# A mixture-of-experts layer in which 32 of 256 tokens take their down products from gathered rows on VectorE

## The chip, the core and the metric

The kernel runs on one core of a Trainium2 chip. The metric is the device time in microseconds of one execution, the median of several. TensorE (PE, with PEld for its weight loads), VectorE (DVE), ScalarE (ACT), GpSimd (POOL) and the queue of SyncE (SP) each run their own instructions in order and wait for one another by semaphores.

## The reference, cut to what matters

Two transformer blocks over 256 tokens of width 1024. The first ends with PEER, a retrieval of experts, which the change is about:

```
sub_scores = einsum('thpc,hpkc->thpk', qry, sub_keys)   # 8 heads x 2 halves x 128 keys
top_s, top_i = top_k(sub_scores, 16)                    # 32 searches of 128 per token tile pair
best_s, best_c = top_k(sums of 16 x 16 pairs, 16)       # 8 heads: 128 experts per token
gate = softmax(best_s)
u = expert_down[ids]                                    # 128 of 16384 rows, each 1024 wide
act = gelu(einsum('pd,ped->pe', x, u)) * gate
y = einsum('pe,ped->pd', act, expert_up[ids])
```

## The kernel before

The retrieval gathers nothing. It multiplies all 256 tokens with all 16384 rows of `expert_down`, in 128 units of 128 rows (`downs`): a unit loads 512 KB (`wst`), splits it into a rounded part on ACT (`whi`, L78) and a rest on DVE (`wlo`, L80), and PE runs 24 matmuls, three for each of eight slices of the width, into a PSUM tile `dn` of 128 x 256 (`mm3`, L113 to L115; the tokens are `hh` and `hl`, split likewise). `wst`, `whi` and `wlo` have three buffers each. ACT puts gelu of `dn` into `G[:, j, :]`.

The choice of experts becomes a gate matrix. `tops` and `select` search on DVE (`top16`, five instructions; 32 searches over 128 keys, then 16 over 136 pair sums, a token tile being 128 tokens), turn pair numbers into indices by one-hot blocks (L730 on ACT, L731 to L738 on DVE), and `softmax` transposes indices and gates to `ijgT`. `gates` takes four tokens at a time: ACT builds `A` and DVE `B` (one-hot rows, `B` times the gate), PE multiplies them into `gp`, and DVE multiplies the units of G that are there with it; units that come later are multiplied in `downs`. `ups` then multiplies G with all of `expert_up`, into `y`.

Three generators set the order: queries and the first 44 units beside the searches; 80 units beside the 64 gate batches; the last 4 beside `ups`. `interleave` takes from the stream that is least far. A scheduler of the tile framework then sets each engine's order by what it expects an instruction to cost; on the chip each engine follows that order.

Of the kernel before, what the change touches and what calls it, by code (L numbers as in the profile page):

```python
# [8 lines left out]
F32 = mybir.dt.float32  # L9
F32R = mybir.dt.float32r  # L10
BF16 = mybir.dt.bfloat16
I32 = mybir.dt.int32
U16 = mybir.dt.uint16
AF = mybir.ActivationFunctionType
OP = mybir.AluOpType
# [28 lines left out]
def interleave(*streams):  # L44


    gens = [[e[0], e[1], e[2] if len(e) > 2 else 0.0] for e in streams]
    while gens:
        gens.sort(key=lambda e: e[2])
        e = gens[0]  # L50
        try:
            e[2] += (next(e[0]) or 1.0) / e[1]
        except StopIteration:
            gens.remove(e)


class Core:
# [15 lines left out]
    def unit(self, ap, n=1024):  # L73
        nc = self.nc
        st = self.wst.tile([P, 1024], F32, tag="wst", name="wst")
        nc.sync.dma_start(st[:, :n], ap)
        hi = self.whi.tile([P, 1024], F32R, tag="whi", name="whi")
        self.last_hi = nc.scalar.activation(hi[:, :n], st[:, :n], AF.Copy)  # L78
        lo = self.wlo.tile([P, 1024], F32R, tag="wlo", name="wlo")
        nc.vector.tensor_tensor(lo[:, :n], st[:, :n], hi[:, :n], OP.subtract)  # L80
        return hi, lo

    def unit_hi(self, ap):
# [76 lines left out]
    def rsqrt(self, pool, ms, scale, n, tag, tiles=None):  # L160

        nc = self.nc
        p = ms.shape[0]
        r, t = tiles or [pool.tile([P, n], F32, tag=tag + x, name=tag + x) for x in "rt"]
        self.act_le(r[:p], ms, AF.Ln, scale=scale, bias=self.eps[:p])
        self.act_le(r[:p], r[:p], AF.Exp, scale=-0.5)

        self.rs_act = nc.scalar.activation(t[:p], r[:p], AF.Square, scale=float(np.sqrt(0.5 * scale)))
        nc.vector.scalar_tensor_tensor(t[:p], ms, EPS / scale, t[:p], OP.add, OP.mult)
        self.rs_dve = nc.vector.scalar_tensor_tensor(r[:p], t[:p], 1.5, r[:p], OP.subtract, OP.mult, reverse0=True)  # L170
        return r[:p]

# [412 lines left out]


    def peer(self):
        nc, a = self.nc, self.a
        h = (self.hh, self.hl)
        with ExitStack() as st:  # L590
            pg = self.pool("pg", 1, stack=st)
            tm = self.pool("pgt", 2, stack=st)
# [38 lines left out]
            nc.vector.tensor_copy(iob, self.iota[:, :16])  # L631
            ijgT = [pg.tile([P, T], F32, name=f"ijgT{x}") for x in range(3)]

            def downs(js, state):
                for j in js:
                    w = self.unit(a["down"][j])
                    ps = dps.tile([P, T], F32, tag="d", name="dn")
                    self.mm3(ps, w, h)
                    b = 4 * state["batches"]
                    if b == 0:  # L640
                        nc.scalar.activation(G[:, j, :], ps, AF.Gelu)  # L641
                    else:
                        t = tm.tile([P, T], F32, tag="gel", name="gel", bufs=1)
                        if b < T:
                            nc.scalar.activation(G[:, j, b:], ps[:, b:], AF.Gelu)
                        self.last_gelu = nc.scalar.activation(t[:, :b], ps[:, :b], AF.Gelu)
                        nc.vector.tensor_tensor(G[:, j, :b], G[:, j, :b], t[:, :b], OP.mult)
                    state["downs"] = j + 1
                    yield

            def queries():
                def scores(hp):
                    q = qry[hp % 2]
                    sp = gps.tile([P, 512], F32, tag="g", name="sp")
                    for tt in range(2):
                        nc.tensor.matmul(sp[:, tt * P:(tt + 1) * P], q[:, tt * P:(tt + 1) * P], subk[:, hp, :], start=True, stop=True)
                    for tt in range(2):
                        nc.scalar.activation(S[tt][:, hp, :], sp[:, tt * P:(tt + 1) * P], AF.Copy)

                first = []  # L660
                for hp in range(2):
                    first.append((dps.tile([P, T], F32, tag="d", name="qp"), self.unit(a["wq"][hp])))
                self.mm3s(first, h)
                for hp in range(16):
                    if hp < 2:
                        ps = first[hp][0]
                    else:
                        w = self.unit(a["wq"][hp])
                        ps = dps.tile([P, T], F32, tag="d", name="qp")
                        self.mm3(ps, w, h)  # L670
                    nc.scalar.activation(qry[hp % 2], ps, AF.Copy)
                    if hp:
                        scores(hp - 1)
                    yield
                scores(15)

# [25 lines left out]
            def select():  # L702
                for tt in range(2):
# [23 lines left out]
                    for s in range(2):  # L727
                        if s == 0:
                            yield 3.0
                        self.after(nc.scalar.activation(abx, ab[s].unsqueeze(3).broadcast_to([P, 8, 16, 16]), AF.Copy), self.last_hi)  # L730
                        nc.vector.tensor_tensor(eq, abx,  # L731
                                                iob.unsqueeze(1).unsqueeze(1).broadcast_to([P, 8, 16, 16]), OP.is_equal)
                        yield 2.2
                        nc.vector.tensor_tensor(eq, eq, idxb[tt][:, :, s, :].unsqueeze(2).broadcast_to([P, 8, 16, 16]), OP.mult)

                        for w in (8, 4, 2):
                            nc.vector.tensor_tensor(eq[:, :, :, :w], eq[:, :, :, :w], eq[:, :, :, w:2 * w], OP.add)
                        nc.vector.tensor_tensor(ijg[tt][s].rearrange("p (h k) -> p h k", h=8), eq[:, :, :, 0], eq[:, :, :, 1], OP.add)  # L738
                        yield 2.4
                    g = ijg[tt][2].rearrange("p (h k) -> p h k", h=8)  # L740
                    nc.vector.tensor_tensor(g, best[tt], best[tt][:, :, 0:1].broadcast_to([P, 8, 16]), OP.subtract)
                    if tt:
# [4 lines left out]
            def gates(state):  # L747
                iT, jT, gT = ijgT
                for b in range(T // 4):
                    gp = gps.tile([P, 4, P], F32, tag="g", name="gp")  # L750

                    A = tm.tile([P, 4, P], F32, tag="A", name="A", bufs=3)
                    for q in range(4):
                        nc.scalar.activation(A[:, q, :], self.iota, AF.Abs, bias=iT[:, 4 * b + q:4 * b + q + 1])  # L754
                    nc.scalar.activation(A, A, AF.Relu, bias=1.0, scale=-1.0)
                    for q in range(4):
                        t = 4 * b + q
                        B = tm.tile([P, P], F32, tag="B", name="B", bufs=4)
                        nc.vector.tensor_scalar(B, self.iota, jT[:, t:t + 1], gT[:, t:t + 1], OP.is_equal, OP.mult)  # L759
                        nc.tensor.matmul(gp[:, q, :], A[:, q, :], B, start=True, stop=True)  # L760
                    gv = gp.rearrange("p t j -> p j t")
                    n = state["downs"]
                    ts = slice(4 * b, 4 * b + 4)
                    if n:
                        nc.vector.tensor_tensor(G[:, :n, ts], G[:, :n, ts], gv[:, :n, :], OP.mult)
                    if n < NS:
                        nc.scalar.activation(G[:, n:, ts], gv[:, n:, :], AF.Copy)
                    state["batches"] = b + 1
                    yield
# [33 lines left out]
            def take(g, n):  # L803
                for _ in range(n):
                    try:
                        next(g)
                    except StopIteration:
                        return
                    yield
# [9 lines left out]
            interleave((chain(qs, take(dn, self.cfg["sel"])), 14.0 + self.cfg["sel"]), (chain(tops(), select()), 80.0))  # L819
            for x in range(3):  # L820
                self.dump(f"ijgT{x}", ijgT[x])
            interleave((take(dn, self.cfg["gate"]), float(self.cfg["gate"])), (gates(state), 64.0))
            rest = NS - state["downs"]
            def gate2():

# [25 lines left out]
            for c in range(8):  # L851
# [8 lines left out]
                if c == 5:  # L860
                    third = self.unit_hi(a["win2"][0])
            self.pre[0] = self.unit_lo(*third, self.last_hl)
            self.dump("x2", self.xT)
            r = self.rsqrt(None, ms[:, :T], 1.0 / D, T, "", [self.rb, Gf[:, 2 * T:3 * T]])


    def block2(self, peer=True):
# [494 lines left out]
def layouts(i):  # L1362
# [29 lines left out]
    o["subk"] = f("peer_sub_keys").reshape(16, P, P).transpose(2, 0, 1).reshape(P, 2048)  # L1392
    o["down"] = f("peer_down").reshape(P, P, 8, P).transpose(1, 3, 2, 0).reshape(P, P, 1024)
    o["up"] = f("peer_up").reshape(P, P, 1024).transpose(1, 0, 2)
    w = f("w_in_2")
    kv = lambda b: w[:, 512 + 128 * b:640 + 128 * b]

# [29 lines left out]
```

## Time and profile before

| | |
|---|---|
| median of 3 runs | 1391.29 us (1390.59 to 1391.79) |
| the profiled execution | 1389.8 us, span 1388.0 |
| busy PE / PEld / DVE / ACT / POOL | 1353.5 / 1256.4 / 991.9 / 816.9 / 4.6 us |
| mean granted TensorE clock | 0.993 of 2.4 GHz |
| data by DMA | 248.53 MB, 179 GB/s |

The span runs from the first to the last instruction. A busy share is an average; the rows below show the stretches of the retrieval. Matmuls overlap, so a matmul's time in a row is longer than the distance to the next; PE's pace is read from the starts.

### The profile page before, as it was taken

To read this page: it belongs to the slowest core of one execution; us is meant where nothing else is said; L and a number is where in the kernel's file an instruction comes from. 1 tells how busy PE (TensorE), PEld (TensorE's weight loads), DVE (VectorE), ACT (ScalarE), POOL (GpSimd) and SP (SyncE) were. 2 spreads that over 40 slices of the span, in tenths; PEclk is the share of its full clock that TensorE was granted. 3 is DMA by queue.
4 is the path that set the end of the run, shared out by engine and by line. 5 is a ranking of instruction groups with operands and counts; after the bars stand their busy time and mean duration, and the time that the engine had idled before them with its cause. 6 is when DMAs were issued, how large, how long until landed. Compare 5 with 4: busy or idle time off the path is not lost.

```text
span 1388.0 us, 24896 instructions
## 1 busy us (share of the span) xinstructions
PE 1353.5 (98%) x9598; PEld 1256.4 (91%) x9598; DVE 991.9 (71%) x2050; ACT 816.9 (59%) x1577; POOL 4.6 (0%) x17
## 2 busy tenths in 40 slices
PE   6999979999999999999999999999998999999998
PEld 6988879999999999999988888888888988999998
DVE  6788979996766667777776666665667787755555
ACT  3466545446778888888545555455556565644443
POOL 0000000000000000000000000000001000000000
PEclk9999999999999999999999999999999999999999
DMA  8686344456544444444566666566654731455554
GB/s 340 223 318 245 105 150 149 149 179 195 180 154 141 150 152 140 151 152 141 181 212 212 215 211 212 196 195 188 194 178 153 213 122 62 138 186 185 182 185 129
DMA packets 65828, 248.53 MB, mean 179 GB/s; under 512 B 7568, under 2 KB 8464, under 8 KB 62766
## 3 DMA queue, kind: packets, MB, share of 16 engines
q1 hardware_dynamic: 65709, 246.94, 54.2%
q8 instruction: 75, 1.23, 0.4%
q14 instruction: 44, 0.35, 0.1%
HBM read 245.87 MB, written 1.05 MB: 178 GB/s over the span
## 4 chain that ended last, share of the span: by engine, by line
PE 89%; DVE 7%; ACT 2%; DMA 1%; issue 1%; SPq 0%; DVEq 0%; ACTq 0%
PE y L785 8%; PE y L787 8%; PE y L786 8%; PE dn L113 8%; PE dn L114 8%; PE dn L115 8%; PE gp L760 4%; DVE wlo L80 2%; PE fu L115 2%; PE fu L114 2%; PE fu L113 2%; PE yf L1287 2%; PE yf L1288 2%; PE yf L1289 2%; PE pj L113 2%; PE pj L115 2%
## 5 line engine op out<-in xcount | busy, mean ns | idle before, releaser
L80 DVE TENSOR_TENSOR wlo<-wst,whi 128x1024 fp32r<-128x1024 f32 (+1 forms) x410 | 499.9, 1220 | 203.1 <-ACT whi L78 202.4
L78 ACT ACTIVATE whi<-wst 128x1024 fp32r<-128x1024 f32 (+1 forms) x410 | 431.1, 1052 | 261.2 <-PE dn L114 77.0
L113 PE MATMUL dn<-hh,whi 128*128 128x256 f32 x1024 | 295.8, 289 | 1.1 <-ACT G L641 1.1
L115 PE MATMUL dn<-hh,wlo 128*128 128x256 f32 x1024 | 290.2, 283 | 2.8 <-DVE wlo L80 2.8
L114 PE MATMUL dn<-hl,whi 128*128 128x256 f32 x1024 | 289.5, 283 | 0.0
L785 PE MATMUL y<-whi,aa 128*128 128x512 f32 x512 | 200.0, 391 | 0.0
L787 PE MATMUL y<-whi,aa 128*128 128x512 f32 x512 | 199.3, 389 | 0.0
L786 PE MATMUL y<-wlo,aa 128*128 128x512 f32 x512 | 199.3, 389 | 0.0
L115 PEld LDWEIGHTS dn<-hh,wlo 128*128 128x128 f32 x1024 | 195.9, 191 | 3.7 <-DVE wlo L80 3.6
L113 PEld LDWEIGHTS dn<-hh,whi 128*128 128x128 f32 x1024 | 196.2, 192 | 1.7 <-ACT G L641 1.5
L114 PEld LDWEIGHTS dn<-hl,whi 128*128 128x128 f32 x1024 | 196.3, 192 | 0.1
L775 ACT ACTIVATE aa<-G 128x256 fp32r<-128x256 f32 x128 | 53.3, 418 | 142.7 <-PE y L787 142.4
L787 PEld LDWEIGHTS y<-whi,aa 128*128 128x128 f32 x512 | 96.1, 188 | 20.2
L786 PEld LDWEIGHTS y<-wlo,aa 128*128 128x128 f32 x512 | 96.2, 188 | 19.7
L785 PEld LDWEIGHTS y<-whi,aa 128*128 128x128 f32 x512 | 96.2, 188 | 19.4
L759 DVE TENSOR_SCALAR B<-cst,ijgT,ijgT 128x128 f32<-128x128 f32 x256 | 71.5, 343 | 55.4 <-PE gp L760 54.5
L776 DVE TENSOR_TENSOR aa<-G,aa 128x256 fp32r<-128x256 f32 x128 | 54.1, 424 | 51.2 <-ACT aa L775 51.0
L754 ACT ACTIVATE A<-cst,ijgT 128x128 f32<-128x128 f32 x256 | 88.2, 399 | 0.0
L115 PE MATMUL pj<-hh,wlo 128*128 128x256 f32 x240 | 70.0, 293 | 3.9 <-DVE wlo L80 3.8
L114 PE MATMUL fu<-hl,whi 128*128 128x256 f32 x256 | 72.6, 284 | 0.0
L113 PE MATMUL fu<-hh,whi 128*128 128x256 f32 x256 | 72.6, 284 | 0.0
L115 PE MATMUL fu<-hh,wlo 128*128 128x256 f32 x256 | 72.5, 283 | 0.0
(410 smaller groups left out, 2619.0 us busy)
## 6 DMA issues: line engine op xcount, KB each, us to landing
wst<-in_down SPq DMA_DIRECT2D x128, 512.0 KB, 3.5
wst<-in_up SPq DMA_DIRECT2D x128, 512.0 KB, 3.5
ada<-in_ada SPq DMA_DIRECT2D x20, 1024.0 KB, 8.3
wst<-in_win SPq DMA_DIRECT2D x40, 512.0 KB, 4.2
wst<-in_wup SPq DMA_DIRECT2D x32, 512.0 KB, 3.5
wst<-in_wdn SPq DMA_DIRECT2D x32, 512.0 KB, 3.5
wst<-in_wq SPq DMA_DIRECT2D x16, 512.0 KB, 3.6
wst<-in_wqk SPq DMA_DIRECT2D x8, 512.0 KB, 6.6
```

The source lines that it names most:

```text
L78: self.last_hi = nc.scalar.activation(hi[:, :n], st[:, :n], AF.Copy)
L80: nc.vector.tensor_tensor(lo[:, :n], st[:, :n], hi[:, :n], OP.subtract)
L113: nc.tensor.matmul(ps, wh[:, s], xh[:, k, :], start=first, stop=False, skip_group_check=shared)
L114: nc.tensor.matmul(ps, wh[:, s], xl[:, k, :], start=False, stop=False, skip_group_check=shared)
L115: nc.tensor.matmul(ps, wl[:, s], xh[:, k, :], start=False, stop=(n == len(order) - 1), skip_group_check=shared)
L754: nc.scalar.activation(A[:, q, :], self.iota, AF.Abs, bias=iT[:, 4 * b + q:4 * b + q + 1])
L759: nc.vector.tensor_scalar(B, self.iota, jT[:, t:t + 1], gT[:, t:t + 1], OP.is_equal, OP.mult)
L760: nc.tensor.matmul(gp[:, q, :], A[:, q, :], B, start=True, stop=True)
L776: nc.vector.tensor_tensor(al, G[:, j, :], ah, OP.subtract)
L785: nc.tensor.matmul(y[tt][c], ah[:, ts], wh[:, s], start=(j == 0), stop=False)
L786: nc.tensor.matmul(y[tt][c], ah[:, ts], wl[:, s], start=False, stop=False)
L787: nc.tensor.matmul(y[tt][c], al[:, ts], wh[:, s], start=False, stop=(j == NS - 1))
```

## The change

The first 32 tokens leave `downs`. Its matmuls take the other 224 tokens (`hd`, `TD`); the instruction count stays. For the 32 tokens, `row_index` turns the chosen indices into row numbers, laid out as 32 groups of 128 rows (32 tokens times 4 picks on the partitions). `rows` gathers each group from `downr`, a copy of `expert_down` in row order, by an indirect DMA on POOL's queue into one of two buffers, and DVE multiplies it with the tokens `xs` and sums (`dot`). A transpose, gelu and a product with the gates follow; the last eight gate batches are those of the 32 tokens and write G instead of multiplying it. The two buffers are `xT`, whose content waits in the PSUM tiles of `y` (`token_rows`) and is copied back at the end of `rows`. `rows` runs beside the gate batches, each dot behind the split made last. Two instructions get an order by hand (`rs_dve0` behind the third split at the next block's start).

```diff
 def peer(self):
+    TS, TD = 32, T - 32
+    R = P // TS
+    NG = P // R
+    hd = (self.hh[:, :, TS:], self.hl[:, :, TS:])
...
+    xrow = [self.xT[:, 4 * q:4 * q + 4, :].rearrange("p k t -> p (k t)") for q in range(2)]
+    def token_rows():
+        for b in range(4):
+            nc.scalar.activation(yb[b], self.xT[:, 2 * b:2 * b + 2, :], AF.Copy)
+        nc.vector.tensor_tensor(xrow[0].rearrange("p (k r t) -> p k r t", k=KT, r=R),
+                                self.hh[:, :, 0:TS].unsqueeze(2).broadcast_to([P, KT, R, TS]),
+                                self.hl[:, :, 0:TS].unsqueeze(2).broadcast_to([P, KT, R, TS]), OP.add)
+        for b in range(2):
+            ps = gps.tile([P, 512], F32, tag="g", name="xsp")
+            for k in range(4):
+                nc.tensor.transpose(ps[:, k * P:(k + 1) * P], xrow[0][:, (4 * b + k) * P:(4 * b + k + 1) * P], self.ident)
+            nc.scalar.activation(xs[:, b * 512:(b + 1) * 512], ps, AF.Copy)
+    def rows():
+        for g in range(NG):
+            u = xrow[g % 2]
+            nc.gpsimd.indirect_dma_start(out=u, out_offset=None, in_=a["downr"], in_offset=bass.IndirectOffsetOnAxis(ap=rowi[:, g:g + 1], axis=0))
+            dot = nc.vector.scalar_tensor_tensor(u, u, 1.0, xs, OP.mult, OP.mult, accum_out=sact[:, g:g + 1])
+            self.after(dot, self.last_lo)
+            yield
...
+        nc.vector.tensor_tensor(ijgT[2][:, :TS], ijgT[2][:, :TS], actT, OP.mult)
+        for b in range(4):
+            nc.scalar.activation(self.xT[:, 2 * b:2 * b + 2, :], yb[b], AF.Copy)
...
-                    ps = dps.tile([P, T], F32, tag="d", name="dn")
-                    self.mm3(ps, w, h)
+                    ps = dps.tile([P, T], F32, tag="d", name="dn")[:, :TD]
+                    self.mm3(ps, w, hd)
...
+                    if hp == 8:
+                        token_rows()
...
+                    t0 = (4 * b + TS) % T
-                    n = state["downs"]
-                    ts = slice(4 * b, 4 * b + 4)
+                    n = state["downs"] if t0 >= TS else 0
+                    ts = slice(t0, t0 + 4)
...
-            interleave((take(dn, self.cfg["gate"]), float(self.cfg["gate"])), (gates(state), 64.0))
+            interleave((take(dn, self.cfg["gate"]), float(self.cfg["gate"])), (gates(state), 64.0), (rows(), 42.0))
...
+            self.after(self.rs_dve0, third_lo)
```

On DVE, near the end of the searches (MAX, MAX_INDEX and MATCH_REPLACE are the searches, the tiles `G` their scratch, L80 is a unit's split), before:

```order
L687 MAX G<-G 128x8
L685 MAX_INDEX G<-G 128x8
L688 MAX_INDEX G<-G 128x8
L684 MAX G<-G 128x8
L686 MATCH_REPLACE G<-G 128x136
L80 TENSOR_TENSOR wlo<-wst,whi 128x1024
L687 MAX G<-G 128x8
L685 MAX_INDEX G<-G 128x8
```

In the change, the last split among the searches, the searches' end, and what follows (L785 and later is a one-hot block):

```order
L740 MATCH_REPLACE G<-G 128x136
L80 TENSOR_TENSOR wlo<-wst,whi 128x1024
L741 MAX G<-G 128x8
L742 MAX_INDEX G<-G 128x8
L797 TENSOR_TENSOR G<-G 128x128
L773 CAST G<-G 128x128
L774 TENSOR_SCALAR G<-G 128x128
L775 TENSOR_SCALAR G<-G 128x128
L80 TENSOR_TENSOR wlo<-wst,whi 128x1024 x13
L785 TENSOR_TENSOR G<-G 128x2048
L776 CAST G<-G 128x128
L788 TENSOR_TENSOR G<-G 128x2048
```

Counted over the whole stretch, between the 28th and the 48th search stand 14 splits before and 3 in the change; 13 moved behind the searches, into one block.

On DVE, early in the gate batches (L759 makes `B`, L765 is the product with `gp`, L647 the product with a later unit), before:

```order
L765 TENSOR_TENSOR G<-G,gp 128x46x4
L647 TENSOR_TENSOR G<-G,gel 128x4
L80 TENSOR_TENSOR wlo<-wst,whi 128x1024
L759 TENSOR_SCALAR B<-cst,ijgT_2038,ijgT_2039 128x128 x4
L765 TENSOR_TENSOR G<-G,gp 128x47x4
```

In the change (L817, L823 and L699 are the same three, L674 is the dot product):

```order
L823 TENSOR_TENSOR G<-G,gp 128x47x4
L817 TENSOR_SCALAR B<-cst,ijgT_2038,ijgT_2039 128x128
L80 TENSOR_TENSOR wlo<-wst,whi 128x1024
L674 SCALAR_TENSOR_TENSOR xT,sact<-xT,xs 128x1024
L817 TENSOR_SCALAR B<-cst,ijgT_2038,ijgT_2039 128x128 x3
L699 TENSOR_TENSOR G<-G,rb 128x12
L823 TENSOR_TENSOR G<-G,gp 128x48x4
```

A dot stands behind a split in about two of three batches, ahead of the next batch's `B` and products.

## Rows read from the trace of the kernel before

**Rows 1.** The page: the span, and busy time by engine.
```profile
span 1388.0 us, 24896 instructions
...
PE 1353.5 (98%) x9598; PEld 1256.4 (91%) x9598; DVE 991.9 (71%) x2050; ACT 816.9 (59%) x1577; POOL 4.6 (0%) x17
```

**Rows 2.** The page: the chain that ended last, by engine.
```profile
PE 89%; DVE 7%; ACT 2%; DMA 1%; issue 1%; SPq 0%; DVEq 0%; ACTq 0%
```

**Rows 3.** Windows: busy PE, PEld, DVE, ACT, POOL; clock; DMA share; GB/s.
```profile
251.00:303.00 52.00, 48.15 (x388) 46.65 (x387) 51.52 (x223) 23.27 (x37) 0.00 (x0) 1.00 0.49 157
303.00:389.00 86.00, 86.00 (x714) 85.48 (x714) 57.72 (x73) 57.58 (x90) 0.00 (x0) 1.00 0.60 188
389.00:671.00 282.00, 282.00 (x2392) 282.00 (x2391) 202.63 (x474) 232.45 (x604) 0.00 (x0) 1.00 0.45 147
```

**Rows 4.** Windows of tile `dn` alone: busy PE, PEld, ACT.
```profile
251.00:292.39 41.39, 36.49 (x288) 35.04 (x288) 4.06 (x11) 1.00 0.48 154
292.39:388.70 96.31, 96.27 (x791) 95.67 (x792) 12.12 (x33) 1.00 0.60 186
```

**Rows 5.** Tile `gp`: duration min/median/max in ns, first and last start.
```profile
L760 PEld LDWEIGHTS gp<-B,A x512: 190/192/192, 388.7 to 670.0; 128*128 128x128 f32 x171
```

**Rows 6.** Timeline of PE: start, duration; the first and last of eight `dn`.
```profile
320.23 0.28 PE L113 MATMUL dn<-hh,whi 128*128 128x256 f32 x1
...
321.07 0.28 PE L114 MATMUL dn<-hl,whi 128*128 128x256 f32 x1
```

**Rows 7.** Timeline of PE: the first and last of five `y`.
```profile
899.74 0.39 PE L786 MATMUL y<-wlo,aa 128*128 128x512 f32 x1
...
900.65 0.39 PE L787 MATMUL y<-whi,aa 128*128 128x512 f32 x1
```

**Rows 8.** Timeline: `adap` matmuls of 32 columns, and the loads of `gp`.
```profile
16.44 1.42 PE L276 MATMUL adap<-silb,ada 128*128 128x32 f32 x12
...
503.95 0.98 PEld L760 LDWEIGHTS gp<-B,A 128*128 128x128 f32 x8
```

**Rows 9.** Timeline of DVE: the first and third of three splits among searches.
```profile
246.53 1.21 DVE L80 TENSOR_TENSOR wlo<-wst,whi 128x1024 fp32r<-128x1024 f32 x1
...
253.74 1.21 DVE L80 TENSOR_TENSOR wlo<-wst,whi 128x1024 fp32r<-128x1024 f32 x1
```

**Rows 10.** Line 688, the searches' last instruction: first and last start.
```profile
L688 DVE FIND_INDEX8 G<-G x48: 280/287/298, 211.6 to 302.7; 128x8 uint16<-128x128 f32 x32, 128x8 uint16<-128x136 f32 x16
```

**Rows 11.** Timelines of ACT and DVE: the pieces of one-hot blocks.
```profile
305.69 1.90 ACT L730 ACTIVATE G<-G 128x2048 bf16<-128x2048 bf16 x1
...
307.62 1.23 DVE L731 TENSOR_TENSOR G<-G 128x2048 bf16<-128x2048 bf16 x1 [0.53 <-ACT G L730]
...
310.73 1.22 DVE L734 TENSOR_TENSOR G<-G 128x2048 bf16<-128x2048 bf16 x1
...
323.63 1.61 DVE L737 TENSOR_TENSOR G<-G 128x1024 bf16<-128x1024 bf16 x3
325.27 0.42 DVE L738 TENSOR_TENSOR G<-G 128x128 f32<-128x128 bf16 x1
```

**Rows 12.** Windows near the start, columns as in rows 3.
```profile
17.00:24.00 7.00, 4.21 (x22) 3.88 (x22) 6.33 (x18) 3.03 (x7) 0.00 (x0) 0.69 1.03 421
24.00:31.00 7.00, 7.00 (x52) 7.00 (x52) 4.86 (x12) 2.22 (x3) 0.00 (x0) 0.83 0.98 376
```

**Rows 13.** Lines 254 and 765: durations in ns, first and last start.
```profile
L254 DVE SCALAR_TENSOR_TENSOR adacc<-ada,silu_c,adacc x42: 740/752/754, 63.9 to 162.3; 128x512 f32<-128x512 f32 x42
...
L765 DVE TENSOR_TENSOR G<-G,gp x64: 335/496/659, 390.3 to 670.8; 128x180 f32<-128x180 f32 x1, 128x184 f32<-128x184 f32 x1, 128x188 f32<-128x188 f32 x1, 128x192 f32<-128x192 f32 x1
```

**Rows 14.** Waits from 389 to 671: us in total, times, longest.
```profile
DVE B L759 <- PE gp L760: 54.5, 63, 1.3
```

**Rows 15.** The page: DMA issues, KB each, median us to landing.
```profile
wst<-in_down SPq DMA_DIRECT2D x128, 512.0 KB, 3.5
```

More of the change, by code (lines that the diff above doesn't have):

```diff
@@ L79, in unit @@
         lo = self.wlo.tile([P, 1024], F32R, tag="wlo", name="wlo")
-        nc.vector.tensor_tensor(lo[:, :n], st[:, :n], hi[:, :n], OP.subtract)
+        self.last_lo = nc.vector.tensor_tensor(lo[:, :n], st[:, :n], hi[:, :n], OP.subtract)
         return hi, lo
@@ L168, in rsqrt @@
         self.rs_act = nc.scalar.activation(t[:p], r[:p], AF.Square, scale=float(np.sqrt(0.5 * scale)))
-        nc.vector.scalar_tensor_tensor(t[:p], ms, EPS / scale, t[:p], OP.add, OP.mult)
+        self.rs_dve0 = nc.vector.scalar_tensor_tensor(t[:p], ms, EPS / scale, t[:p], OP.add, OP.mult)
         self.rs_dve = nc.vector.scalar_tensor_tensor(r[:p], t[:p], 1.5, r[:p], OP.subtract, OP.mult, reverse0=True)
@@ L632, in peer @@
             ijgT = [pg.tile([P, T], F32, name=f"ijgT{x}") for x in range(3)]
+            xs = pg.tile([P, D], F32, name="xs")
+            rowf = pg.tile([P, NG], F32, name="rowf")
+            rowi = pg.tile([P, NG], I32, name="rowi")
+            sact = pg.tile([P, NG], F32, name="sact")
+            actT = pg.tile([P, TS], F32, name="actT")
+            xrow = [self.xT[:, 4 * q:4 * q + 4, :].rearrange("p k t -> p (k t)") for q in range(2)]
[10 more added lines that the diff above has]
+                    nc.scalar.activation(xs[:, b * 512:(b + 1) * 512], ps, AF.Copy)
@@ new lines, in row_index @@
+            def row_index():
+                w = tm.tile([P, P], F32, tag="B", name="rowx", bufs=4)
+                nc.vector.scalar_tensor_tensor(w[:TS], ijg[0][1][:TS], float(P), ijg[0][0][:TS], OP.mult, OP.add)
+                for r in range(R):
+                    nc.scalar.activation(rowf[r * TS:(r + 1) * TS, :], w[0:TS, r * NG:(r + 1) * NG], AF.Copy)
+                nc.vector.tensor_copy(rowi, rowf)
+            def rows():
[5 more added lines that the diff above has]
+                    yield
+                tp = gps.tile([P, 512], F32, tag="g", name="tps")
+                nc.tensor.transpose(tp[:NG, :P], sact, self.ident)
+                for r in range(R):
+                    nc.scalar.activation(actT[r * NG:(r + 1) * NG, :], tp[:NG, r * TS:(r + 1) * TS], AF.Gelu)
+                nc.vector.tensor_tensor(ijgT[2][:, :TS], ijgT[2][:, :TS], actT, OP.mult)
+                for b in range(4):
+                    nc.scalar.activation(self.xT[:, 2 * b:2 * b + 2, :], yb[b], AF.Copy)
+                yield
@@ L636, in downs @@
                     w = self.unit(a["down"][j])
-                    ps = dps.tile([P, T], F32, tag="d", name="dn")
-                    self.mm3(ps, w, h)
-                    b = 4 * state["batches"]
+                    ps = dps.tile([P, T], F32, tag="d", name="dn")[:, :TD]
+                    self.mm3(ps, w, hd)
+                    b = min(4 * state["batches"], TD)
                     if b == 0:
-                        nc.scalar.activation(G[:, j, :], ps, AF.Gelu)
+                        nc.scalar.activation(G[:, j, TS:], ps, AF.Gelu)
                     else:
-                        t = tm.tile([P, T], F32, tag="gel", name="gel", bufs=1)
-                        if b < T:
-                            nc.scalar.activation(G[:, j, b:], ps[:, b:], AF.Gelu)
+                        t = self.rb[:, :TD]
+                        if b < TD:
+                            nc.scalar.activation(G[:, j, TS + b:], ps[:, b:], AF.Gelu)
                         self.last_gelu = nc.scalar.activation(t[:, :b], ps[:, :b], AF.Gelu)
-                        nc.vector.tensor_tensor(G[:, j, :b], G[:, j, :b], t[:, :b], OP.mult)
+                        nc.vector.tensor_tensor(G[:, j, TS:TS + b], G[:, j, TS:TS + b], t[:, :b], OP.mult)
                     state["downs"] = j + 1
@@ L739, in select @@
                         yield 2.4
+                    if tt == 0:
+                        row_index()
                     g = ijg[tt][2].rearrange("p (h k) -> p h k", h=8)
@@ L753, in gates @@
                     for q in range(4):
-                        nc.scalar.activation(A[:, q, :], self.iota, AF.Abs, bias=iT[:, 4 * b + q:4 * b + q + 1])
+                        nc.scalar.activation(A[:, q, :], self.iota, AF.Abs, bias=iT[:, t0 + q:t0 + q + 1])
                     nc.scalar.activation(A, A, AF.Relu, bias=1.0, scale=-1.0)
                     for q in range(4):
-                        t = 4 * b + q
+                        t = t0 + q
                         B = tm.tile([P, P], F32, tag="B", name="B", bufs=4)
@@ L862, in peer @@
             self.pre[0] = self.unit_lo(*third, self.last_hl)
+            third_lo = self.last_lo
             self.dump("x2", self.xT)
             r = self.rsqrt(None, ms[:, :T], 1.0 / D, T, "", [self.rb, Gf[:, 2 * T:3 * T]])
+            self.after(self.rs_dve0, third_lo)
     def block2(self, peer=True):
@@ L1394, in layouts @@
     o["up"] = f("peer_up").reshape(P, P, 1024).transpose(1, 0, 2)
+    o["downr"] = f("peer_down").reshape(P, P, 1024).transpose(1, 0, 2).reshape(P * P, 1024)
     w = f("w_in_2")
```

## The prediction

> **What bounds the kernel now.** I read the page first, then the busy times of the retrieval by stretch, then single instructions. The page gives the PE 98% of a span of 1388.0 us and DVE 71% [rows 1]; the chain that ended last is PE for 89% and DVE for 7% [rows 2]. So only what shortens or idles the PE counts. By stretch [rows 3]: from 251 to 303 DVE is busy 51.52 of 52 us (the top-16 searches) and PE 48.15; from 303 to 671 PE is never idle, while DVE has 57.7 of 86 and 202.6 of 282. The search stretch is therefore balanced on two engines, and the rest is PE's. Before 292.39 the PE ran 288/24 = 12 units of `dn`, and 33 more up to the first gate matmul at 388.7 [rows 4, 5].
>
> **Term 1, the narrower matmul.** Eight `dn` matmuls of 256 columns start over 0.84 us: 0.120 each [rows 6]. Five `y` matmuls of 512 columns start over 0.91: 0.2275 each [rows 7]. The difference, 0.1075 for 256 columns, makes 0.0134 for 32, so that by columns alone 224 would take 0.1066. But each matmul has a weight load of 128 columns. The one place where the columns can't be the limit is `adap`, with 32: its 12 matmuls start over 1.42 - 0.28 = 1.14 us, or 0.104, and the eight loads of `gp` over 0.98 - 0.19 = 0.79, or 0.113 [rows 8]. I take 0.112 as the load's floor, nearest to `gp`, which stands among the `dn` matmuls; ends: 0.104 (no floor that matters) and 0.120 (nothing gained). So a unit goes from 24 x 0.120 = 2.88 us to 2.69, not to 2.56.
>
> The Trainium skill weighs in on both sides here. "TensorE: Matmul & The Clock Gate", section "Back-to-back issue gap", has the gap as the columns over 2.4 GHz plus 2.5 ns: an estimate of 96 ns for 224, by which the 78 units of the gate stretch would win 45 us. Its section "LDWEIGHTS (loading the stationary operand)" has a load as its columns over 1.2 GHz, 107 ns for 128, whatever streams: 24 us. The rows side with the load, and add 5 ns to it.
>
> **Term 2, the search stretch.** The order shows what no row of time does: up to the 28th of the 48 searches both programs have split the weights of three `dn` units. From there to the 48th search DVE has 14 more splits (`wlo`) before, and 3 in the change; its next 13 stand in one block behind the search. DVE runs in order, so PE gets three units in that time instead of fourteen. Two searches and a split take (253.74 - 246.53)/2 = 3.6 us, of it 1.2 the split [rows 9]. The search thus ends 11 x 1.2 = 13.2 us before the 303.0 of the last index search [rows 10], plus 1.2 for the new sum of `hh` and `hl` (1024 elements, a split's length): at about 291. PE has then run 6 units, and starts the seventh behind the next split, at 292; before, it had run 12 by 292.39. From there 39 units x 2.69 = 104.9 and 1.3 for the rest (96.31 less 33 x 2.88 in [rows 4]) bring the first gate matmul to 398.2 instead of 388.7: **+9.5**.
>
> Then the four one-hot blocks of the selection. Before, a split stands between their pieces; now a block is whole. The wide copy on ACT takes 1.90, the comparison 1.23, the product 1.22, three halvings 1.61, the last sum 0.42 [rows 11]: 6.4 us without a split, and 2.3 more until the next `whi` and `wlo` are made. Three buffers of each let PE run one to two units (2.7 to 5.4 us) ahead, so a block costs 3.3 to 6.0; four cost 13 to 24, and nothing if the lead turns out three units. I take 4.5 each: **+18**. Where these gaps are long, the clock can fall: in the stretch from 17 to 24 us, where PE was busy for 4.21 of 7, the granted clock is 0.69 (a mix of 1.2 and 2.4 GHz), and 0.83 in the 7 us behind it, full of work [rows 12]. That is a loss of 1.2 us for one gap, hidden where PE waits anyway; for two or three: **+3** (0 to 7).
>
> **Term 3, the gate stretch.** 45 units lie ahead of the first gate matmul, 78 between it and the last at 670.0 [rows 5], 5 behind. 78 x 24 x 0.008 = **-15**, and **-1** for the five. The gate matmuls stay. What hides the new work there: a dot product is a three-operand pass over 1024 elements; that form takes 0.752 for 512 [rows 13], a plain pair 1.21 for 1024 [rows 9], so about 1.3, from 1.2 to 1.5. 32 x 1.3 = 42 us on DVE; the last eight batches drop their product (0.66 each [rows 13]), -5. DVE goes from 202.6 to 239 of now 267 us, 89%, and ACT, with four copies back to `xT` and eight wide evictions, from 232.5 [rows 3] to some 238. DVE has the room because it waits 54.5 us for gate matmuls to free `B` [rows 14]; behind a waiting dot stand the next split, the gate's `B` and the products with G, for which PE waits. Cost taken: **+1**, up to +10 if DVE's rest is not where the dots are.
>
> Each row transfer waits on POOL for the dot two before it. 32 of them in 33/42 of 267 us make 6.6 us a row, so from one dot to the use of the buffer it frees there are 13.1 us less the dot: it may take 11.9 us. The nearest row, a load of the same 512 KB on SP's queue, lands in 3.5 [rows 15]. POOL's queue holds only memsets and a cast of the next block behind them, free at 0.8 of the stretch. SP's queue keeps its order but for two loads at the next block's start, now behind five small ones: 0 to 2 us, taken as 0. The Trainium skill ("DMA: Bandwidth & Descriptors", "Anatomy of one DMA") gives 2.0 us and the bytes over 436 KB a us for a transfer from POOL, an estimate of 3.2 us here; no run shows it.
>
> **Sum.** 9.5 + 18 + 3 - 15 - 1 + 1 = +15.5 on the profiled run of 1389.8 (span 1388.0): 1405.3. The median shown stands 1.5 above that run, so **1407 us**. With the block price and the clock at their ends this case spans 1395 to 1418.
>
> **Rivals.**
> - *No gain per matmul* (0.120 stays, because the load with its hand-over fills it): term 2 grows by 39 x 0.19 = 7.5, term 3 loses its 16: 1407 + 23 = 1430, or 1426 with blocks better covered by the slower PE. For it: `dn` sits at 0.120 with PEld 282 of 282 us busy [rows 3]. Against: `gp` at 0.113. 10%.
> - *Columns alone count*, 0.1066: 39 x 0.13 = -5 and 83 x 0.13 = -11: 1391 to 1397, DVE then at 93%. 9%.
> - *Row transfers late.* Above 11.9 us a transfer, two buffers pace the stretch: at 14 us a row takes 7.65 instead of 6.6, 32 x 1.05 = +34: 1440. It decides from 12 us. Against it, 3.5 us [rows 15]. 8%.
> - *Narrow products in this number form run at four passes.* Every such matmul of the trace has 256 columns or more (256 and 512 in [rows 6, 7]), so no row excludes it. 224 x 4/2.4 + 13 = 387 ns, 128 x 24 x 0.267 = +820: about 2200. The order of splits, three units to 20 searches (25 us), is what a planner would write that held a unit for 9 us. 6%.
> - *The other side: faster.* If PE is not starved, because the splits' place costs nothing (the lead of three units covers every gap), there remain 33 + 83 units x 0.19 = -22: 1369. It needs PE to have work at 260 to 290 us, which the in-order splits refuse; it decides where the search stretch loses under 15 us in all, of the 30 that I sum. 7%.
>
> **How the numbers follow.** My case has 60%: 1407. Faster by over 0.2% (2.8 us, what a measurement here can tell from no change) is the last rival and a little of the second: 0.09. Within 0.2%: the upper part of the second, 0.05. Slower: 0.86. The range 1392 to 1440 takes my case, most of the second rival, the first, and half of the third: 8 in 10.
>
> **What would show it.** `dn` starts 0.112 apart; PE idle in stretches of 6 to 9 us between 258 and 292, waiting for `wlo`; the first `gp` at 410 to 420 rather than 388.7; a gate stretch of about 267 to 270 us rather than 282, DVE near 90% in it; dots of 1.3 us, row transfers landing well within 10. I am wrong if `dn` stays at 0.120 or falls to 0.107, if PE is busy from 258 to 292, or if dots wait for DMA.

## The result, and the profile after

The changed kernel takes 1407.26 us (median of 4 runs, 1406.93 to 1409.32) against 1391.54 before (1390.59 to 1393.94): a ratio of 1.0113, interval 1.0096 to 1.0131, 15.7 us slower. The profiled execution took 1407.5. Its page, the lines that answer to [rows 1]:

```profile
span 1405.7 us, 25044 instructions
...
PE 1339.5 (95%) x9607; PEld 1241.4 (88%) x9607; DVE 1029.0 (73%) x2110; ACT 820.2 (58%) x1585; POOL 39.4 (3%) x49
```

PE is busy 14.0 us less in a span 17.7 us longer: it idles 66.2 us instead of 34.5. Where, the windows say (columns as in [rows 3]); below them tile `dn` alone up to 292.39 (columns as in [rows 4]):

```profile
251.00:303.00 52.00, 33.31 (x228) 32.36 (x226) 46.57 (x220) 13.88 (x25) 0.00 (x0) 0.77 0.28 93
303.00:389.00 86.00, 77.05 (x661) 75.94 (x660) 46.75 (x56) 50.01 (x84) 2.93 (x2) 0.96 0.55 177
389.00:671.00 282.00, 277.45 (x2474) 276.32 (x2474) 243.80 (x530) 238.81 (x606) 31.88 (x30) 1.00 0.68 213
...
251.00:292.39 41.39, 19.80 (x123) 18.91 (x123) 1.71 (x5) 0.76 0.19 65
```

In the search stretch PE runs 123 `dn` matmuls, five units, where it ran 288, and the granted clock is 0.77 instead of 1.00. The gate matmuls, against [rows 5]:

```profile
L818 PEld LDWEIGHTS gp<-B,A x512: 187/192/193, 418.1 to 686.5; 128*128 128x128 f32 x171
```

The first comes at 418.1 instead of 388.7 (+29.4), and from first to last they take 268.4 us instead of 281.3 (-12.9). From the last to the end it is 719.2 instead of 718.0 (+1.2). That sums to the 17.7 of the spans.

PE's timeline shows the two mechanisms. First, inside the gate stretch, the first and last of eight neighbouring `dn` matmuls (start, duration):

```profile
502.02 0.28 PE L114 MATMUL dn<-hl,whi 128*128 128x224 f32 x1
...
502.80 0.28 PE L115 MATMUL dn<-hh,wlo 128*128 128x224 f32 x1
```

Seven distances in 0.78 us are 0.111 each; it was 0.120 [rows 6]. Second, between 258 and 350 us, the matmuls that end the long gaps (in brackets the idle time before, and what ended it), with one matmul further on in the same unit:

```profile
270.60 0.56 PE L115 MATMUL dn<-hh,wlo 128*128 128x224 f32 x1 [7.14 <-DVE wlo L80]
...
275.22 0.41 PE L115 MATMUL dn<-hh,wlo 128*128 128x224 f32 x1
...
281.13 0.56 PE L115 MATMUL dn<-hh,wlo 128*128 128x224 f32 x1 [5.12 <-DVE wlo L80]
...
292.28 0.55 PE L115 MATMUL dn<-hh,wlo 128*128 128x224 f32 x1 [5.87 <-DVE wlo L80]
...
346.62 0.56 PE L113 MATMUL dn<-hh,whi 128*128 128x224 f32 x1 [5.87 <-ACT G L693]
```

Three gaps wait for a split (`wlo`) that stands behind searches on DVE. The fourth has another cause, which ACT's timeline shows:

```profile
337.43 1.90 ACT L784 ACTIVATE G<-G 128x2048 bf16<-128x2048 bf16 x1
344.30 0.95 ACT L667 ACTIVATE rowf<-rowx 32x32 f32<-32x32 f32 x4 [4.97 <-DVE rowx L665]
345.27 1.06 ACT L78 ACTIVATE whi<-wst 128x1024 fp32r<-128x1024 f32 x1
```

ACT's four copies of the row numbers wait 4.97 us until DVE is through a one-hot block, and the next unit's rounded part, which needs nothing of DVE, stands behind them. The releaser named on PE, `ACT G`, is only ACT's last event before; ACT's own queue corrects it.

### The profile page after: what moved, and what is told of

It reads as the page before. It is cut to its first block, busy times and chain, and to the rows that moved or that the text cites. A ratio compares the mean times of both kernels' runs of the same rounds, so it can differ in the third digit from the quotient of the medians.

```text
span 1405.7 us, 25044 instructions
## 1 busy us (share of the span) xinstructions
PE 1339.5 (95%) x9607; PEld 1241.4 (88%) x9607; DVE 1029.0 (73%) x2110; ACT 820.2 (58%) x1585; POOL 39.4 (3%) x49
## 4 chain that ended last, share of the span: by engine, by line
PE 67%; DVE 3%; ACT 3%; DMA 2%; issue 1%; DVEq 0%; ACTq 0%
PE y L845 8%; PE y L843 8%; PE y L844 8%; PE dn L113 6%; PE dn L114 6%; PE dn L115 6%; PE gp L818 4%; PE fu L115 2%; PE fu L114 2%; PE fu L113 2%; PE yf L1347 2%; PE yf L1348 2%; PE yf L1349 2%; ACT whi L78 1%; PE ops L1231 1%; DVE wlo L80 1%
## 5 line engine op out<-in xcount | busy, mean ns | idle before, releaser
L80 DVE TENSOR_TENSOR wlo<-wst,whi 128x1024 fp32r<-128x1024 f32 (+1 forms) x410 | 499.3, 1220 | 211.4 <-ACT whi L78 209.5
L115 PE MATMUL dn<-hh,wlo 128*128 128x224 f32 x1024 | 285.8, 279 | 19.5 <-DVE wlo L80 19.5
L113 PE MATMUL dn<-hh,whi 128*128 128x224 f32 x1024 | 290.9, 284 | 7.9 <-ACT G L693 7.8
L114 PE MATMUL dn<-hl,whi 128*128 128x224 f32 x1024 | 284.8, 278 | 0.0
L115 PEld LDWEIGHTS dn<-hh,wlo 128*128 128x128 f32 x1024 | 201.0, 196 | 20.4 <-DVE wlo L80 20.4
L113 PEld LDWEIGHTS dn<-hh,whi 128*128 128x128 f32 x1024 | 201.2, 196 | 8.9 <-ACT G L693 8.8
L114 PEld LDWEIGHTS dn<-hl,whi 128*128 128x128 f32 x1024 | 201.0, 196 | 0.1
L817 DVE TENSOR_SCALAR B<-cst,ijgT,ijgT 128x128 f32<-128x128 f32 x256 | 76.7, 341 | 14.7 <-PE gp L818 13.8
L113 PE MATMUL pj<-hh,whi 128*128 128x256 f32 x240 | 70.9, 295 | 3.7 <-DVE qraw L1041 3.7
```

Source lines behind the costliest of these rows:

```text
L80: self.last_lo = nc.vector.tensor_tensor(lo[:, :n], st[:, :n], hi[:, :n], OP.subtract)
L113: nc.tensor.matmul(ps, wh[:, s], xh[:, k, :], start=first, stop=False, skip_group_check=shared)
L114: nc.tensor.matmul(ps, wh[:, s], xl[:, k, :], start=False, stop=False, skip_group_check=shared)
L115: nc.tensor.matmul(ps, wl[:, s], xh[:, k, :], start=False, stop=(n == len(order) - 1), skip_group_check=shared)
```

## The experiments

**The splits put back.** DVE's instructions of the searches and the selection are tied to the places that they have before among the splits. Only DVE's queue is tied; the planner sets the others anew, and on ACT one `whi` that stood behind the copies of the row numbers now stands ahead of them.

```diff
+    places = [n for n, c in ((6, 28), (7, 5), (8, 5), (9, 10), ...) for _ in range(c)]
+    class Placed:          # stands for nc.vector in tops, top16, softmax and select
+        ...
+        i = getattr(nc.vector, op)(*args, **kw)
+        n = min(places[count[0]], len(self.los) - first_lo)
+        self.after(i, self.los[first_lo + n - 1])   # behind the n-th split
```

> The changed kernel, but each search and selection instruction on DVE is tied behind the split that it follows in the kernel before (a table of places in the queue); nothing else differs. Theory A (the place of the splits starves PE): PE is busy from 258 to 292 us again. Before, 16 units had started when the last search ended at 303; DVE is full there, so that stays. The other 29 units at 2.69 us and 1.3 us for the rest bring the first gate matmul to 383 us, or up to 393 where the selection's blocks, no shorter than before, no longer fit beside the faster units. Gate stretch 268 us as in the changed kernel. Sum: 1407.3 less (418.1 - 388) = 1377, from 1371 to 1383. Theory B (what costs before the gates is the new work there: the token sum, the row index and their waits): the order gives back 8 us at most: 1399 to 1407, first gate matmul still after 410.

1384.43 us (1383.69 to 1384.58), ratio to before 0.9952, 0.9937 to 0.9967: 22.8 less than the changed kernel, and 1.4 above my range. Its search stretch in the windows, and its gate matmuls (tile `gp`):

```profile
251.00:303.00 52.00, 47.77 (x405) 45.81 (x403) 51.42 (x219) 23.02 (x37) 0.00 (x0) 1.00 0.51 162
```

```profile
L836 PEld LDWEIGHTS gp<-B,A x512: 186/192/192, 394.7 to 663.1; 128*128 128x128 f32 x171
```

PE is fed again (405 matmuls for 228) and the clock is 1.00. Theory A holds for most of the loss; 394.7 against 388.7 leaves 6 us open, which B may claim. One gap longer than 1.1 us is left ahead of the gates:

```profile
326.91 0.56 PE L115 MATMUL dn<-hh,whi 128*128 128x224 f32 x1 [3.45 <-ACT G L695]
```

**All 256 columns, the rest of the change kept.**

```diff
-    ps = dps.tile([P, T], F32, tag="d", name="dn")[:, :TD]
-    self.mm3(ps, w, hd)
+    ps = dps.tile([P, T], F32, tag="d", name="dn")
+    self.mm3(ps, w, h)
+    ps = ps[:, TS:]
```

> The changed kernel, but its dn products take all 256 tokens again (the 32 columns too many are not used); row gathers, dots and gates stay as in the change. Theory A (the planner moves the splits because of the number of columns): the splits stand among the searches as before, dn starts 0.120 us apart, the first gate matmul is at 390 us, the gate stretch 282 to 285, sum 1391.5 + 1.5 + 2 = 1395, from 1390 to 1400. Theory B (the new work costs, not the columns): the loss of 29 us before the gates stays and the 24 us that narrow products win go: about 1430.

1392.69 us (1390.93 to 1395.85), ratio 1.0010, 1.0000 to 1.0019. The splits stand among the searches with no order by hand (the same two views):

```profile
251.00:303.00 52.00, 49.66 (x402) 48.38 (x401) 51.42 (x222) 23.13 (x38) 0.00 (x0) 1.00 0.49 155
```

```profile
L819 PEld LDWEIGHTS gp<-B,A x512: 190/192/192, 389.3 to 670.7; 128*128 128x128 f32 x171
```

So the number of columns makes the planner move the splits; the row work, which is all there, doesn't. On the chip a narrow product is shorter, not longer, so the planner's order does not fit it. What the planner expects of either width was not read.

**The row work left out.** `token_rows`, `row_index` and `rows` aren't called.

> The changed kernel without the row work: no token sum, no row numbers, no gathers, no dots, no product with the gates (so the 32 tokens' values are left out); the narrow products, the order of the gate batches and all else stay. Theory A: the row work costs 1.2 us of DVE in the searches and about 2 us in the gate stretch: 1404, from 1399 to 1407, first gate matmul at 414 to 418. Theory B (the row work is the cause of the loss): 1376 to 1390, first gate matmul before 395.

1397.70 us (1394.97 to 1400.21), ratio 1.0052, 1.0038 to 1.0065: 9.6 less than the changed kernel, more than A's 3 and less than B's 17.

```profile
L814 PEld LDWEIGHTS gp<-B,A x512: 192/192/192, 411.7 to 677.8; 128*128 128x128 f32 x171
```

By the profiled spans (1405.7 and 1395.4) it is 10.3: 6.4 lie ahead of the first gate matmul (418.1 to 411.7), 2.3 in the gate stretch (268.4 to 266.1) and 1.6 behind it, where both kernels do the same work. The three gaps in the searches stay without the row work: 8.34, 5.08 and 5.71 us. Both theories were off: the row work is the smaller part, but not small.

**Fewer columns still,** in the order by hand:

```diff
-    self.mm3(ps, w, hd)
+    for n in range(3 * KT):
+        k, e = n // 3, n % 3
+        c = TD if n == 0 else 192
+        nc.tensor.matmul(ps[:, :c], w[e // 2][:, k * P:(k + 1) * P], hd[e % 2][:, k, :c], start=(n == 0), stop=(n == 3 * KT - 1))
```

> The kernel with the order by hand, but 23 of each unit's 24 dn products take 192 instead of 224 columns (so 32 more tokens lack most of their sum); loads, counts and evictions stay. Theory A (a matmul that streams few columns waits for the next weight load of 128 columns): dn starts stay 0.112 us apart, and the time is that of the order by hand within 2 us, by my sum 1377. Theory C (columns alone, 192/2.4 + 13.3 = 93 ns): 83 units win 24 x 0.0187 us each, 37 us, until DVE, busy for 234 of 268 us, is the bound: 1340 to 1352, dn starts 0.093 to 0.100 apart.

1383.29 us (1380.77 to 1386.25), against 1384.43 with 224. Eleven neighbouring matmuls, the first and the last:

```profile
500.80 0.28 PE L695 MATMUL dn<-hl,whi 128*128 128x192 f32 x1
...
501.92 0.27 PE L695 MATMUL dn<-hh,wlo 128*128 128x192 f32 x1
```

Ten distances in 1.12 us: 0.112. Columns stopped counting somewhere between 256 and 224, and 32 fewer are worth nothing. Theory C falls. The time is within 2 us of the order by hand, as Theory A had it.

**The row numbers' copies later on ACT,** once in the order by hand and once in the changed kernel.

```diff
     # called at softmax(0) of the second token tile instead of behind the first tile's selection
-    nc.scalar.activation(rowf[r * TS:(r + 1) * TS, :], ...)
+    self.after(nc.scalar.activation(rowf[r * TS:(r + 1) * TS, :], ...), self.last_hi)
```

DVE's cast of the row numbers (0.18 us) moves with them.

> The order by hand, and ACT's four copies of the row numbers (line 667 of the changed kernel) are tied behind the split of the unit issued last when the second token tile's searches are half done, instead of standing ahead of the next unit's split on ACT. Theory D (those copies wait on ACT for DVE's one-hot block, 5.0 us in the changed kernel, and the next unit's rounded part waits behind them): PE's gap of 3.72 us at 323 goes, the first gate matmul comes 4 us earlier, at 390 to 391: 1384.4 - 4 = 1380, from 1378 to 1382. Rival (the gap is DVE's own work in the block): no change, 1383 to 1386, the gap still there.

1378.43 us (1376.96 to 1379.39), ratio 0.9905, 0.9887 to 0.9923: the fastest kernel here that computes everything, 6.0 less than the order by hand. The gap at 323 is gone: no gap ahead of the gates is longer than 1.2 us. The gate matmuls:

```profile
L840 PEld LDWEIGHTS gp<-B,A x512: 186/192/192, 389.2 to 657.6; 128*128 128x128 f32 x171
```

> The changed kernel with only ACT's row-number copies moved to the later place; the splits stand as in the change. Theory D: the gap of 6.1 us at 340 shrinks by the 5 us of the copies' wait, and the unit behind it is not slowed: first gate matmul at 413, 1407.3 - 5 = 1402, from 1400 to 1404. Rival (the block has no split in it whatever ACT does, so the gap stays): 1406 to 1408.

1401.37 us (1399.54 to 1402.68), ratio 1.0069, 1.0054 to 1.0084: 5.9 less than the changed kernel, first gate matmul at 413.3. The gap at 340 shrinks from 5.87 to 1.80 us, and the unit behind it runs at the full clock:

```profile
345.48 0.37 PE L115 MATMUL dn<-hh,wlo 128*128 128x224 f32 x1 [1.80 <-DVE wlo L80]
```

```profile
L822 PEld LDWEIGHTS gp<-B,A x512: 186/192/192, 413.3 to 681.7; 128*128 128x128 f32 x171
```

Theory D holds in both: of the 6.4 us that the row work costs before the gates, this wait on ACT is 4.8 (418.1 to 413.3). The rest of the 5.9 lies behind the last gate matmul, where nothing differs.

**Columns and row work in the good order.**

> The order by hand with dn products of all 256 tokens again: the same queue places, only the columns differ. Theory A: dn starts 0.120 us apart again; the 83 units from the first gate matmul on lose 24 x 0.008 each, 16 us, of which DVE's waiting gives nothing back; ahead of it DVE and ACT set most of the pace and 2 to 4 us are lost: 1384.4 + 18 = 1402 if the blocks are as badly covered as with 224, 1393 if the slower PE hides them. Rival (the narrow products' gain is taken back by the dots on DVE): within 4 us of the order by hand, 1384 to 1388.

1392.10 us (1390.13 to 1394.62), ratio 1.0007, 0.9998 to 1.0017. The gate stretch:

```profile
L837 PEld LDWEIGHTS gp<-B,A x512: 190/192/192, 389.1 to 670.5; 128*128 128x128 f32 x171
```

281.4 us instead of 268.4 with 224 columns: 13.0, the gain of the narrow products beside the dots. So the rival falls, and of Theory A's two sums the second, 1393, holds. The gap at 323 that the copies made with 224 columns is not there, and ACT's queue says why: the copies' line in the order by hand, and here:

```profile
324.58 0.95 ACT L669 ACTIVATE rowf<-rowx 32x32 f32<-32x32 f32 x4 [4.94 <-DVE rowx L667]
...
326.27 0.95 ACT L669 ACTIVATE rowf<-rowx 32x32 f32<-32x32 f32 x4 [0.46 <-DVE rowx L667]
```

Between the one-hot block's wide copy on ACT and these copies stands one `whi` in the order by hand and none in the changed kernel; with 256 columns there are three, so the copies come when DVE is almost through the block. DVE's places were tied, ACT's weren't: the number of columns moves ACT's queue too. With all 256 columns and nothing tied (the second experiment) the copies also wait 0.5 us, and there the whole change costs 1.5 us.

> The order by hand without the row work (no token sum, row numbers, gathers, dots or product with the gates; the 32 tokens' values are left out). Theory D: the copies' wait of 4 us, the token sum's 1 us and 2.3 us in the gate stretch go: 1384.4 - 7.5 = 1377, from 1374 to 1379, gate stretch 266. Rival (the row work's cost before the gates belongs to the starved order alone): 1381 to 1384.

1373.37 us (1371.70 to 1375.88), 11.1 less than the order by hand, some more than D's 7.5 and 0.6 below its range; the rival falls. Its stretch is 266.1 us:

```profile
L832 PEld LDWEIGHTS gp<-B,A x512: 192/192/192, 390.0 to 656.1; 128*128 128x128 f32 x171
```

Against the kernel with the late copies 5.1 us remain for the row work by the medians. The profiled spans, 1377.0 and 1374.1, show 2.9 of them, 2.3 in the stretch; the rest is unexplained.

**Which half of the order.**

```diff
-    if n:
+    if 0 < n < 33:     # the searches; the other kernel: if n >= 33, the selection
         self.after(i, self.los[first_lo + n - 1])
```

> The order by hand, but only the places of the searches are tied (all that stand ahead of the 33rd split); the selection's blocks stand where the planner puts them. The full order by hand gave back 22.9 us. Theory P (the terms of the prediction, 9.5 for the searches and 21 for the blocks and the clock): the searches' places give back a third of that, 7 us: 1400, from 1398 to 1402. Theory T (the trace of the changed kernel: the seventh unit starts at 296.7, 4.7 us later than I had summed, and the 39 units behind it lose 15 and not 21): they give back 14 of it and the slow clock between the searches: 15 us, 1392, from 1389 to 1395. First gate matmul at 411 by P, at 402 to 404 by T.

1390.11 us (1388.76 to 1392.55), ratio 0.9991, 0.9982 to 1.0001: 17.2 less than the changed kernel.

```profile
L836 PEld LDWEIGHTS gp<-B,A x512: 186/192/192, 400.7 to 669.3; 128*128 128x128 f32 x171
```

> The other half: only the places of the selection's instructions (from the 33rd split on) are tied; the searches run with few splits as in the change. Theory P: two thirds of the 22.9 us come back, 15: 1392, from 1390 to 1395. Theory T: 8 us come back, 1399, from 1396 to 1402, since the row numbers' copies still hold ACT and PE still gets its seventh unit at 296.7; first gate matmul at 409 to 411.

1402.35 us (1400.64 to 1402.64), ratio 1.0073, 1.0057 to 1.0090: 4.9 less.

```profile
L836 PEld LDWEIGHTS gp<-B,A x512: 186/192/192, 412.4 to 681.2; 128*128 128x128 f32 x171
```

Theory T is the nearer in both, with more on the side of the searches than it had: the first gate matmuls, 400.7 and 412.4, lie 1.3 and 1.4 us outside its ranges and the second time 0.35 us above. The halves add to 22.1 of the 22.8. In the second half the gap at the copies is 3.43 us instead of 5.87, for there too ACT has a `whi` ahead of them; so about 2.4 of its 4.9 us are that wait and not the blocks.

## Why the prediction was right, and where only its sum was

**The narrower matmul, right.** 0.112 was taken between 0.104 and 0.120; it is 0.111 to 0.112, and it is a floor that columns don't set, since 192 give the same. The other end, 0.104 from `adap`, was misread: that row's first two matmuls start 0.03 us apart (16.44 and 16.46), and from the second on eleven start over 1.39 - 0.28 = 1.11 us, 0.111 each, with 32 columns (both lines from the kernel before):

```profile
16.46 1.39 PE L276 MATMUL adap<-silb,ada 128*128 128x32 f32 x11
...
1142.24 0.51 PE L1072 MATMUL vvp<-w,hT 128*15 128x64 f32 x6
```

The second line has loads of 15 columns, and its six matmuls start 0.06 us apart. So it is no floor under every matmul, and it fits the load, as taken; no run changed the load of `dn`, so that the load sets it is the reading and not shown. Without the row work the gate stretch is 266.1 against 281.3, 15.2 less, where the sum had 78 x 24 x 0.008 = 15. The Trainium skill ("TensorE: Matmul & The Clock Gate", section "LDWEIGHTS (loading the stationary operand)") puts a load of 128 columns at an estimated 107 ns; the rows measure 4 to 5 ns more. The formula of the Trainium skill's section "Back-to-back issue gap" that the prediction used, 96 ns, is given there for an isolated matmul; the same section says that in a stream of loads and matmuls both set the distance, so it was no rule against the load, and 0.111 decides.

**The stretch before the gates: right in the sum, wrong in its terms.** 9.5 + 18 + 3 = 30.5; measured 29.4. But the seventh unit starts at 296.7, not at 292, and the 39 behind it lose 418.1 - 296.7 - 106.2 = 15.2, not 21. Three steps failed and cancelled, and a count in the first was off by one:
- *"PE has then run 6 units".* It had run five and two matmuls of the sixth, whose split came only at 291.01:

```profile
279.88 1.20 DVE L80 TENSOR_TENSOR wlo<-wst,whi 128x1024 fp32r<-128x1024 f32 x1
...
291.01 1.22 DVE L80 TENSOR_TENSOR wlo<-wst,whi 128x1024 fp32r<-128x1024 f32 x1
```

  I counted splits made, as if PE had a unit ready with each; a unit that waits for its split ends 2.7 us behind it. And the clock, which I put at the blocks and hid at the searches, costs here, where PE is last: the sixth unit runs at half clock from 292.3 to 296.3. The searches' places, with the slow clock between them, were worth 17.2 us, not 9.5.

  The count: by the traces 13 splits before and 3 in the change stand between the 28th and the 48th search, not 14 and 3 (the split behind the 28th, at 257.35 and 257.89, is the third of the three that both have). The searches end 10 splits earlier, not 11; their last instruction starts at 292.6 [rows 10 has 302.7], and the sum had their end at 291:

```profile
L742 DVE FIND_INDEX8 G<-G x48: 279/287/300, 210.4 to 292.6; 128x8 uint16<-128x128 f32 x32, 128x8 uint16<-128x136 f32 x16
```

- *"I take 4.5 each" for the one-hot blocks.* Two of the four cost PE starts 0.98 and 0.91 us apart (at 331.7 and 390.0 us), one nothing over 0.5 right behind it; I take it that the three buffers' lead covered the rest. Undoing the blocks gave 4.9 us, not 18, and about 2.4 of these belong to the next point.
- *The row index at nothing but a DVE pass.* I read the new order on DVE and not on ACT, and so missed the one long gap at a block, 5.87 us, and the unit at half clock behind it. It is 4.8 us ahead of the gates by the experiment, 5.9 in the medians. The row work as a whole costs 9.6, of which I had 2. Nor is the wait the row work's own: with 256 columns the same copies wait 0.5 us, so this too is an order that came with the narrower tile.

A total that is right by 1 us thus hid three terms that are each wrong by 7 to 13 (17.2 for 9.5, 4.9 for 18, 9.6 for 2): that hit was luck. The ends named for the sum, 13 to 24 for the blocks and 0 to 7 for the clock, make 1399 to 1417 and not 1395 to 1418; nothing hangs on it. Had I put the two orders side by side on ACT as well, the copies ahead of a `whi` would have stood there.

**The gate stretch, nearly right.** The dot's line (durations in ns), and the gathers' time from issue to landing:

```profile
L674 DVE SCALAR_TENSOR_TENSOR xT<-xT,xs x32: 1211/1217/1222, 410.1 to 613.6; 128x1024 f32<-128x1024 f32 x32
```

```profile
DMA to landing us min/median/max: 4.4/5.2/8.7
```

The waits of `B` in that stretch (us in total, times, longest), and the windows of it:

```profile
DVE B L817 <- PE gp L818: 13.8, 29, 0.8
```

```profile
418.00:687.00 269.00, 267.30 (x2391) 266.91 (x2391) 233.76 (x527) 232.79 (x602) 30.01 (x28) 1.00 0.67 209
```

A dot takes 1.22 us (1.3 taken). DVE is busy for 87% (89% forecast): the dots went into the 54.5 us that DVE had waited for gate matmuls [rows 14], of which 13.8 are left. No dot waited for a transfer: DVE's waits in the stretch are for `gp`, `whi`, `rb` alone. The row work costs 2.3 us here instead of 1. Which of the dots, the transfers and their waits makes these 2.3 wasn't tried one by one. The gain of 1 us behind the last gate matmul didn't show: that part took from 717.6 to 721.0 us in the kernels run here.

**The rivals.** *No gain per matmul* and *columns alone* fall to 0.111 at 224 and 0.112 at 192. *Four passes* falls with them; its remark that a planner with such a belief would order the splits as this one did fits, since 256 columns bring the order back, but what the planner holds was not read. *Row transfers late* would have needed 11.9 us; the longest took 8.7, the median 5.2, where the prediction's estimate from the Trainium skill ("DMA: Bandwidth & Descriptors", "Anatomy of one DMA") was 3.2. *Faster* rested on PE having work from 260 to 290 us, and it idled. In the good order with late copies the kernel is faster, 1378, yet not 1369: its first gate matmul comes at 389.2, as before. The 45 units ahead of the gates gain nothing from narrower matmuls: from 251 us to the gates PE idles 9.8 us there instead of 3.9. I take it that DVE sets the pace, full in the searches (51.42 of 52 us) and with a selection no shorter; that wasn't tried.

## What to carry to other kernels

A change of a tile's shape can move work that it doesn't touch, if a planner sets the queues by what it expects shapes to cost: put the queues of before and after side by side on every engine that feeds the bound, not only the one with most of the new work. An operation of 1 us on an engine with time to spare costs as much as the wait at its place in the queue, if the bound's next input stands behind it. And when a sum comes out right, test its terms one by one before believing it.

## What the runs showed of the hardware

- With weights of 128 columns, matmuls of 224, of 192 and of 32 columns start at the same distance, 0.111 to 0.112 us; 256 is longer, 0.120.
- PE idle for 5 to 7 us comes back at the lower of its two clocks. In the changed kernel the granted clock (the third column from the right) is 0.50 from 266 to 271 us, where PE idles, and stays there for nearly the whole next unit:

```profile
266.00:271.00 5.00, 0.40 (x2) 0.40 (x3) 5.00 (x27) 0.00 (x0) 0.00 (x0) 0.50 0.00 0
271.00:276.00 5.00, 5.00 (x24) 4.80 (x23) 4.76 (x28) 0.54 (x1) 0.00 (x0) 0.52 0.32 107
```

```profile
270.95 0.42 PE L113 MATMUL dn<-hh,whi 128*128 128x224 f32 x1
...
275.65 0.36 PE L114 MATMUL dn<-hl,whi 128*128 128x224 f32 x1
```

  The `dn` matmuls of that unit start 0.214 us apart (22 distances in 275.65 - 270.95 = 4.70), where the full clock has 0.111. The same slow start follows the gap of 3.45 us in the order by hand (matmuls of 0.41 us).
- A gather of 128 rows, 512 KB, by an indirect DMA lands in 5.2 us by the median; the plain loads of the same size in the same kernel in 3.9:

```profile
wst<-in_down SPq DMA_DIRECT2D x128, 512.0 KB, 3.9
```
